# Neighbourhood attention and HGRN2 in one trunk: full-row queries for the low part of odd score tiles, and a last pair of loads in another ring

## The chip, the cores and the metric

The kernel runs on one core of a Trainium2 chip. Time is device microseconds (us) of one execution; the median of three runs before is 2596.82 us (2594.27 to 2599.92).

## What is computed

One layer of an encoder trunk over 2048 tokens of width 1024 (a grid of 32 rows by 64 columns). A modulated layer norm gives `h`; one projection gives the inputs of two branches; their outputs pass one output projection, a residual and a final layer norm. The branch that the change touches most is the neighbourhood attention of 16 heads of 64 channels:

```python
proj = h @ w_in[l]
...
q_row = lax.dynamic_index_in_dim(q, r, axis=2, keepdims=False).reshape(B, H, nqb, NA_KC, dh)
s = jnp.einsum('bhjqd,bhrjcd->bhjqrc', q_row, k_blk).astype(jnp.float32) * scale
...
s = jnp.where(col_mask[:, :, None, :], s + bias[None], -jnp.inf)
p = jax.nn.softmax(s.reshape(B, H, nqb, NA_KC, KR * NA_SPAN), axis=-1)
o = jnp.einsum('bhjqrc,bhrjcd->bhjqd', p, v_blk)
```

The other branch is a bidirectional gated recurrence (HGRN2) of 8 heads of 128 channels, computed in chunks, with an RMS norm and a gate on each head's output.

## The kernel before

**Precision.** An fp32 factor is split into a high part, rounded to fp32r, and the low rest, so that a product takes three matmuls: high by high, high by low, low by high.

**Phases.** The tokens are worked on in two halves of 1024. First the attention of the first half runs, woven with its projections (phase `n0`). Then come the 8 heads of HGRN2, twice (phase `h`): `hgrn` is the work of a head, `hgrn_tail` its rest, which is done one head later. The tail of the last head, with `u == 7` in the second half, runs beside `border_dense`: the projections of head pair 0 of the attention's second half, and before and after them a value projection `vproj` (L291, evacuated by ScalarE at L299). Then comes the attention of the second half (phase `n1`), 8 pairs of heads, `p` = 0 to 7, and at last the output projection (phase `wo`).

**The tail of a head.** In the second half the last state `R` is split into `Rh` and `Rl`, and for each group `g` of 512 tokens of the first half four tiles are loaded: `qh`, `ql`, `o1` and `sg`, all from the ring `cl`, which has four buffers. Three matmuls (L690) give what is added to `o1` (L691, VectorE). `rms_out` squares it (L345, ScalarE), splits the square (L347, L349, VectorE), sums over channels by two matmuls with ones (L354, L355), and scales (L357 to L361). The loads of `g == 1` use the buffers that `g == 0` has left: `o1` the one that L359 reads last, `sg` the one that L361 reads last.

**A score tile.** In the second half a pair has 12 tiles: row groups `R` = 1, 2, 3 (512 queries each) by column blocks `j` = 0 to 3. A tile has two heads (`hh`). A head's 64 channels fill half of the partitions; `KA`, `KB` and `Q` hold the high parts in one half and copies or low parts in the other, so that one matmul over all 128 rows (L1055) gives high by high and low by high. What is missing is the low part of the keys, `KL`. In tiles with even `j` the query operand is `Z`, which holds one head's high queries in 64 rows and zeros in the other 64, so that a matmul over all 128 rows (L1060) gives that head's term alone. In tiles with odd `j` the two heads use 64 rows each (L1062): 64 rows of `Q` and of `KL`, one head in the upper rows and one in the lower. `Z` exists once. `alone` (L780, two copies by ScalarE) refills it for the next row group right after the scores of `j == 2`.

**What follows a tile.** VectorE adds the bias and finds the extreme (L1071), ScalarE takes the exponential (L1076), VectorE divides (L1080, L1081). TensorE transposes the result (L1104), VectorE and ScalarE copy that to SBUF (L1108, L1110), and after each odd tile TensorE forms the weighted sums for two earlier tiles (L1126): pairs of matmuls, each with 64 columns of the array for one head. The gated result goes to `yv` (L1136) and to DRAM (L1137).

**Order of the work.** `weave` steps two generators: `natten_woven` (scores, transposes, sums) and a stream of dense projections (L278 with 512 columns, weights split at L814 and L815). For pair 7 the dense stream is the beginning of the output projection (L1547 to L1549); its weights are loaded at L1502 in pair 6 and in pair 7, and split by ScalarE and VectorE (L1507, L1508); the values of `y` are loaded at L1513 and split at L1539, L1540. `prep_now` and `prep_next` say after which of the 12 tiles a preparation is issued: key pieces (L992 to L994), queries (L976 to L979), values (L1003), gates (L1010, L340, L341, L1012), bias tables. TensorE's order is to be that of the code; ScalarE, VectorE and the DMA queue on SyncE (SP) are put in order by a scheduler, from priorities and its own estimate of when things are ready, except for rows pinned by hand.

Of the kernel before, what the change touches and what calls it, by code (L numbers as in the profile page):

```python
# [11 lines left out]
F32R = mybir.dt.float32r  # L12
# [26 lines left out]
def body(ctx: ExitStack, tc: tile.TileContext, t):  # L39
# [48 lines left out]
    def nm(s):  # L88
        cnt[0] += 1
        return f"{s}_{cnt[0]}"  # L90

    def tl(tag, dt=F32, shape=None):
        if tag in cur["smap"]:
            tag = cur["smap"][tag]
            return sh.tile([P, 512], dt, tag=tag, name=nm(tag), bufs=SH[tag])
        return cur["pool"].tile([P, 512] if shape is None else shape, dt, tag=tag, name=nm(tag), bufs=cur["bufs"].get(tag, 1))
# [4 lines left out]
    def ps(tag="mx"):  # L101
        if tag == "pj":
            return pp.tile([P, 512], F32, tag=tag, name=nm("pj"))
        tag = cur["map"].get(tag, tag)
        return cur["psum"].tile([P, 512], F32, tag=tag, name=nm("ps"), bufs=cur["ps"][tag])
# [237 lines left out]
    def rms_out(u, g, o_sb, sg, tok, rest=False):  # L343
        sq = tl("t")
        act.activation(sq, o_sb, AF.Square)  # L345
        sh_ = tl("rh", F32R)
        dve.tensor_copy(sh_, sq)  # L347
        sl_ = tl("rl", F32R)
        dve.tensor_tensor(sl_, sq, sh_, op=ALU.subtract)  # L349
        yield  # L350
        if rest:
            yield
        pss = ps("ss")
        pe.matmul(pss, ones, sh_, start=True, stop=False)  # L354
        pe.matmul(pss, ones, sl_, start=False, stop=True)  # L355
        r = tl("t")
        act.activation(r, pss, AF.Ln, scale=1.0 / 128.0, bias=eps_rms)  # L357
        act.activation(r, r, AF.Exp, scale=-0.5)
        dve.tensor_mul(r, r, o_sb)  # L359
        yv = tl("t")  # L360
        dve.tensor_tensor(yv, r, sg, op=ALU.mult)  # L361
        dma(yT[u][:, tok:tok + 512], yv)
# [60 lines left out]
    def hgrn(u, half, st, tail):  # L423
# [203 lines left out]
        for _ in tail:  # L627
            pass
        return hgrn_tail(u, half, sgs, ubs, decs, qibs, os_, decb_all)

    HSUM = 54

    def hgrn_tail(u, half, sgs, ubs, decs, qibs, os_, decb_all):

        R = None
        if half == 0:
            ds_ = tl("dsuf", shape=[P, 8])
            pool.memset(ds_[:, 7:8], 1.0)
            for b in range(6, -1, -1):
                dve.tensor_mul(ds_[:, b:b + 1], ds_[:, b + 1:b + 2], decb_all[:, b + 1:b + 2])  # L640
        obs = {}
        for g in (1, 0):
            po = os_[g]
            pend = []
            for b in range(3, -1, -1):
                sl = slice(b * P, (b + 1) * P)
                if R is not None:
                    pend.append((sl, R))
                if half == 0 and g == 0 and b == 0:
                    break  # L650
                rn = tl("Sb", shape=[P, P])
                if R is None:
                    dve.tensor_copy(rn, ubs[g][:, sl])
                else:
                    dve.scalar_tensor_tensor(rn, R, decs[1, g][:, b:b + 1], ubs[g][:, sl], op0=ALU.mult, op1=ALU.add)
                R = rn
            yield
            for sl, r in pend:
                pe.matmul(po[:, sl], r, qibs[1, g][:, sl], start=False, stop=True, skip_group_check=True)
            ob = tl("t")  # L660
            act.activation(ob, po, AF.Copy)
            tk = slice(g * 512, (g + 1) * 512)
            if half == 0:
                dma(op_d[u][:, tk], ob)
                dma(sg_d[u][:, tk], sgs[g])
                qb, qh, ql = tl("t"), tl("cl", F32R), tl("cl", F32R)
                for b in range(4):
                    sl = slice(b * P, (b + 1) * P)
                    dve.tensor_scalar(qb[:, sl], qibs[1, g][:, sl], ds_[:, g * 4 + b:g * 4 + b + 1], 1.0, op0=ALU.mult, op1=ALU.mult)
                act.activation(qh, qb, AF.Copy)  # L670
                dve.tensor_tensor(ql, qb, qh, op=ALU.subtract)
                dma(qb_d[u][:, 0, tk], qh.bitcast(F32))
                dma(qb_d[u][:, 1, tk], ql.bitcast(F32))
            else:
                yield from rms_out(u, g, ob, sgs[g], HALF + g * 512, g == 0)
        if half == 1:
            Rh, Rl = tl("Sb", F32R, [P, P]), tl("Sb", F32R, [P, P])
            dve.tensor_copy(Rh, R)
            dve.tensor_tensor(Rl, R, Rh, op=ALU.subtract)
            for g in range(2):  # L680
                tk = slice(g * 512, (g + 1) * 512)
                qh, ql, o1, sg = tl("cl", F32R), tl("cl", F32R), tl("cl"), tl("cl")
                dma(qh.bitcast(F32), qb_d[u][:, 0, tk])
                dma(ql.bitcast(F32), qb_d[u][:, 1, tk])
                dma(o1, op_d[u][:, tk])
                dma(sg, sg_d[u][:, tk])
                yield
                po = ps("pc")
                for i, (a, b) in enumerate(((Rh, qh), (Rh, ql), (Rl, qh))):
                    pe.matmul(po, a, b, start=i == 0, stop=i == 2)  # L690
                dve.tensor_tensor(o1, po, o1, op=ALU.add)  # L691
                yield from rms_out(u, g, o1, sg, g * 512)
# [340 lines left out]
    class Natten:  # L1033
# [8 lines left out]
        def scores(self, R, j):  # L1042
# [8 lines left out]
            def kv(z):  # L1051
                return keys[z].rearrange("p (r c) -> p r c", c=GW)[:, k0 - self.r_base:k0 - self.r_base + nr, KC[j]:KC[j] + kw]
# [2 lines left out]
                pe.matmul(scs[hh][:, 0:nk], qs[hh], kv(("KA", "KB")[hh]), start=True, stop=False, skip_group_check=True)  # L1055
            for hh in range(2):
                hs_ = slice(hh * 64, hh * 64 + 64)
                if self.half and j % 2 == 0:
                    o = hh * 512 + j * P
                    pe.matmul(scs[hh][:, 0:nk], keys["Z"][:, o:o + P], kv("KL"), start=False, stop=True, skip_group_check=True)  # L1060
                else:
                    pe.matmul(scs[hh][:, 0:nk], qs[hh][hs_], kv("KL")[hs_], start=False, stop=True, skip_group_check=True)  # L1062
# [75 lines left out]


    def prep_now(st):  # L1140
        return {0: [(st.k, 3), (st.k, 4)], 1: [(st.q, 3), (st.gate, 2)], 2: [(st.v, 7), (st.v, 5), (st.v, 6)], 4: [(st.gate, 3), (st.table, "bot", 0)],
                6: [(st.table, "bot", 1)], 7: [(st.table, "bot", 3)]}

# [314 lines left out]
    with psum_phase("n0", NPS), tc.manual_schedule(engines={mybir.EngineType.PE}):  # L1458
        with phase("st", SB_, SMS), tc.manual_schedule(engines={getattr(mybir.EngineType, e) for e in ("PE", "SP", "Activation", "DVE")}):
            raws, feed, first = startup()  # L1460
        with phase("n0", NB0, SM0):
            natten_init(4, 0)
            st = first_half(raws, feed, first)
# [7 lines left out]
    with psum_phase("h", *HPS), phase("h", HB, SMH), tc.manual_schedule(engines={mybir.EngineType.PE}):  # L1471
        hgrn_init()
        tail = iter(())
        for i in range(16):
            half, u = divmod(i, 8)
            if i < 15:
                nxt = hgrn_dense((i + 1) % 8, (i + 1) // 8, i in (6, 7), reload if i == 6 else None)
                tail, st = weave(hgrn(u, half, st, tail), nxt, HTOT, HSUM)
# [133 lines left out]
    with psum_phase("n1", NPS), phase("n1", NB1, SM1), tc.manual_schedule(engines={mybir.EngineType.PE}):  # L1612
        natten_init(4, 1)
        st = st0
# [13 lines left out]
        for u in range(8):  # L1628
# [15 lines left out]
            st = nxt  # L1644
# [77 lines left out]
```

## Time and profile before

| what | value |
|---|---|
| median of three runs | 2596.82 us |
| the profiled execution, its own time | 2596.31 us |
| its span, from the first to the last instruction | 2594.5 us |
| mean granted TensorE clock | 0.995 of full speed |
| attention of the second half with its dense stream (`n1`), by the lines' first and last starts | about 1735 to 2280 us |
| TensorE busy in 1740 to 2270 us | 522.92 of 530 us |

Engines are PE (TensorE), PEld (its weight loads), DVE (VectorE), ACT (ScalarE), POOL (GpSimd) and SP (SyncE, which issues the DMAs). A row of the timeline has the start in us from the span's start, the duration, the engine, the line, the operation and the tiles as out<-in; `x2` means that two equal instructions in a row were merged, and brackets hold the idle time before the row and what ended it. Matmuls are pipelined: one starts while the one before it still drains, so what a matmul costs is read from start to start.

### The profile page before, as it was taken

The numbers are of one execution on the slowest core, as the hardware profiler recorded it, in microseconds if no ns is written. First come the engines' busy times: TensorE is split into PE (matmuls) and PEld (weight loads), VectorE is DVE, ScalarE is ACT, GpSimd is POOL, SyncE is SP. The second block draws the span as 40 slices with busy tenths as digits, with TensorE's granted clock in tenths as the row PEclk, the third lists the DMA queues.
The fourth block names the chain that finished last, engine by engine and source line by source line (L and its number), as shares of the span: only waits on it lengthen the run. The fifth ranks groups of instructions, "written<-read, shape, count | busy, mean of one in ns | idle before, by whom it ended". The sixth has DMA issues, their size and how long they took to land.

```text
span 2594.5 us, 46029 instructions
## 1 busy us (share of the span) xinstructions
PE 2557.3 (99%) x17196; PEld 2154.2 (83%) x17196; DVE 1752.1 (68%) x4394; ACT 1438.9 (55%) x2869; POOL 108.5 (4%) x143
## 2 busy tenths in 40 slices
PE   8999999999999999999999999999999999999998
PEld 6888888878888888888888888898888887788887
DVE  7445545387877778877888787555777778648443
ACT  5533444376666666666766666455777777531110
POOL 0000000000000000000000000000000000032221
PEclk9999999999999999999999999999999999999999
DMA  7566454212122226222222222345455556443331
GB/s 293 143 206 154 143 178 140 90 51 70 66 73 74 66 85 228 83 73 86 80 65 69 82 86 83 120 128 155 123 145 136 147 139 173 132 155 130 96 95 57
DMA packets 230527, 304.79 MB, mean 117 GB/s; under 512 B 29351, under 2 KB 118055, under 8 KB 229159
## 3 DMA queue, kind: packets, MB, share of 16 engines
q1 hardware_dynamic: 230303, 301.85, 37.9%
q8 instruction: 135, 2.21, 0.4%
q14 instruction: 89, 0.73, 0.1%
HBM read 222.37 MB, written 71.18 MB: 113 GB/s over the span
## 4 chain that ended last, share of the span: by engine, by line
PE 94%; DVE 3%; ACT 1%; DMA 1%; issue 0%; SPq 0%; DVEq 0%; ACTq 0%
PE pj L278 51%; PE pj L291 7%; PE ps L1549 4%; PE ps L1547 4%; PE ps L1548 4%; PE ps L1126 3%; PE ps L1104 3%; PE ps L482 2%; PE ps L474 2%; PE ps L1055 2%; PE ps L549 1%; PE ps L278 1%; PE ps L578 1%; PE ps L1062 1%; PE ps L580 1%; PE ps L521 1%
## 5 line engine op out<-in xcount | busy, mean ns | idle before, releaser
L278 PE MATMUL pj<-h,wh 128*128 128x512 f32 x3984 | 1264.7, 398 | 1.5 <-ACT wh L814 1.1
L278 PEld LDWEIGHTS pj<-h,wh 128*128 128x128 f32 x3984 | 721.8, 188 | 149.8 <-issue 10.5
L278 PE MATMUL pj<-h,wl 128*128 128x512 f32 x1992 | 780.3, 392 | 0.0
L278 PEld LDWEIGHTS pj<-h,wl 128*128 128x128 f32 x1992 | 373.8, 188 | 82.4 <-DVE wl L815 0.4
L1076 ACT ACTIVATE pbuf<-pbuf,mx 128x480 f32<-128x480 f32 (+5 forms) x256 | 152.5, 597 | 107.5 <-DVE mx L1071 106.4
L291 PE MATMUL pj<-wh,h 128*128 128x256 f32 x1024 | 197.1, 287 | 2.2 <-ACT vt L299 2.0
L1071 DVE CUSTOM_DVE_ANT_1 pbuf<-ps,bias 128x480 f32<-128x480 f32 (+5 forms) x256 | 129.1, 540 | 98.8 <-PE ps L1062 42.1
L291 PEld LDWEIGHTS pj<-wh,h 128*128 128x128 f32 x1024 | 164.6, 193 | 6.0 <-ACT vt L299 3.3
L269 DVE TENSOR_TENSOR wl<-wr,wh 128x512 fp32r<-128x512 f32 x192 | 131.4, 685 | 46.2 <-ACT wh L268 45.9
L268 ACT ACTIVATE wh<-wr 128x512 fp32r<-128x512 f32 x192 | 120.3, 626 | 73.1 <-PE pj L278 66.7
L291 PE MATMUL pj<-wl,h 128*128 128x256 f32 x512 | 145.6, 284 | 0.0
L1110 ACT ACTIVATE pt<-ps 120x384 f32<-120x384 f32 (+3 forms) x128 | 65.2, 510 | 120.1 <-PE ps L1104 119.9
L1104 PE MATMUL ps<-ident,pbuf 128*128 128x128 f32 (+2 forms) x832 | 112.9, 273 | 4.7 <-DVE pbuf L1081 3.9
L1108 DVE COPY pt<-ps 120x384 f32<-120x384 f32 (+3 forms) x128 | 74.9, 585 | 62.5 <-PE ps L1104 61.6
L1104 PEld LDWEIGHTS ps<-ident,pbuf 128*128 128x128 f32 (+2 forms) x832 | 96.6, 136 | 22.7 <-ACT pbuf L1076 2.5
L468 DVE TENSOR_TENSOR de<-e,de 128x512 f32<-128x512 f32 x64 | 44.2, 691 | 92.9 <-ACT de L467 92.9
L1523 ACT ACTIVATE yh<-yr 128x512 fp32r<-128x512 f32 x52 | 32.7, 628 | 132.4 <-PE ps L1548 115.2
L1596 DVE TENSOR_TENSOR vt<-ps,gt 128x512 f32<-128x512 f32 x24 | 16.5, 692 | 129.9 <-PE ps L1549 129.9
L1081 DVE TENSOR_SCALAR pbuf<-pbuf,mx 128x480 f32<-128x480 f32 (+5 forms) x256 | 101.0, 412 | 3.7
L788 ACT ACTIVATE e<-pj 128x512 f32<-128x512 f32 x97 | 57.8, 596 | 78.9 <-PE pj L278 72.0
L291 PEld LDWEIGHTS pj<-wl,h 128*128 128x128 f32 x512 | 98.8, 193 | 1.0
L840 DVE TENSOR_TENSOR wl<-wr,wh 128x512 fp32r<-128x512 f32 x68 | 46.9, 691 | 69.4 <-ACT wh L839 64.3
(289 smaller groups left out, 4771.2 us busy)
## 6 DMA issues: line engine op xcount, KB each, us to landing
wr<-in_w_in SPq DMA_DIRECT2D x276, 256.0 KB
yr<-yq SPq DMA_DIRECT2D x64, 256.0 KB
bias<-tint SPq DMA_DIRECT2D x24, 480.0 KB
x<-in_x SPq DMA_DIRECT2D x32, 256.0 KB
ada<-in_ada_m SPq DMA_DIRECT2D x8, 1024.0 KB
wr<-in_w_v SPq DMA_DIRECT2D x32, 256.0 KB
nv<-vt SPq DMA_DIRECT2D x32, 256.0 KB
hs<-s SPq DMA_DIRECT2D x32, 256.0 KB
```

Source lines behind the costliest of these rows:

```text
L268: act.activation(hi, raw, AF.Copy)
L269: dve.tensor_tensor(lo, raw, hi, op=ALU.subtract)
L278: pe.matmul(pz, a, b, start=(k == 0 and n == 0), stop=(k == KT - 1 and n == 2))
L291: pe.matmul(pzs[tp][:, i * 256:(i + 1) * 256], a, b, start=(k == 0 and n == 0 and i == 0), stop=(k == KT - 1 and n == 2), skip_group_check ...
L1071: return dve.tensor_tensor_reduce(s[:, 0:nk].rearrange("p (r c) -> p r c", c=kw), sc[:, 0:nk].rearrange("p (r c) -> p r c", c=kw), bt[:, 0 ...
L1076: act.activation(s[:, 0:nk], s[:, 0:nk], AF.Exp, scale=-1.0, bias=mx[:, 0:1], accum_out=mx[:, 1:2])
L1081: dve.tensor_scalar(s[:, 0:nk], s[:, 0:nk], mx[:, 2:3], 1.0, op0=ALU.mult, op1=ALU.mult)
L1104: pe.transpose(ptp[0:cw, c * P:(c + 1) * P], s[:, c * cw:(c + 1) * cw], ident)
L1126: pe.matmul(self.po[R][hs_, j * P:(j + 1) * P], v[:, hh * 64:hh * 64 + 64], pts[hh][0:n * KW[j], c * P:(c + 1) * P], start=(c == 0), stop= ...
L1547: pe.matmul(pz, yh[:, kk], wh, start=first, stop=False)
L1548: pe.matmul(pz, yh[:, kk], wl, start=False, stop=False)
L1549: pe.matmul(pz, yl[:, kk], wh, start=False, stop=last)
```

## The change

There are three edits. In the tail of the last head (`u == 7`, `g == 1`) `o1` and `sg` come from the ring `de`, which has two buffers, instead of `cl`. In the second half the odd tiles take the low part with `Z` over all 128 rows, as the even tiles do. For pair 7 `prep_now` issues the gate of row group 2 after tile 3 instead of 1, the queries of row group 3 after tile 5 instead of 1, and the gate of row group 3 after tile 6 instead of 4.

```diff
-                qh, ql, o1, sg = tl("cl", F32R), tl("cl", F32R), tl("cl"), tl("cl")
+                qh, ql = tl("cl", F32R), tl("cl", F32R)
+                o1, sg = (tl("de" if u == 7 and g else "cl") for _ in range(2))
...
-                if self.half and j % 2 == 0:
+                if self.half:
                     o = hh * 512 + j * P
                     pe.matmul(scs[hh][:, 0:nk], keys["Z"][:, o:o + P], kv("KL"), start=False, stop=True, skip_group_check=True)
...
     def prep_now(st):
+        if st.p == 7:
+            return {0: [(st.k, 3), (st.k, 4)], 2: [(st.v, 7), (st.v, 5), (st.v, 6)], 3: [(st.gate, 2)], 4: [(st.table, "bot", 0)], 5: [(st.q, 3)],
+                    6: [(st.gate, 3), (st.table, "bot", 1)], 7: [(st.table, "bot", 3)]}
```

`alone` is left where it was, after the scores of `j == 2`. So in the changed kernel the tile `j == 3` reads a `Z` that already holds the queries of the next row group (except in the very last row group): its product of queries and the keys' low part is taken with other queries than the reference's.

In the changed kernel the lines behind the first edit are numbered one higher (L1060 becomes L1061), and those behind the last edit four higher (L1507 becomes L1511).

The first place is the DMA queue (SP) in the tail of the last head; `cl_18684` to `cl_18687` are the loads for `g == 0`, `cl_18763` on those for `g == 1`, and `wr` are weights of the value projection. Before:

```order
L683 DMA cl_18684<-qb 128x512
L684 DMA cl_18685<-qb 128x512
L685 DMA cl_18686<-op 128x512
L362 DMA yq<-t_18289 128x512
L686 DMA cl_18687<-sgd 128x512
...
L683 DMA cl_18763<-qb 128x512
L684 DMA cl_18764<-qb 128x512
L262 DMA wr_19208<-in_w_v 128x512
L262 DMA wr_19214<-in_w_v 128x512
L685 DMA cl_18765<-op 128x512
L362 DMA yq<-t_18760 128x512
L686 DMA cl_18766<-sgd 128x512
```

And in the changed kernel:

```order
L684 DMA cl_18684<-qb 128x512
L685 DMA cl_18685<-qb 128x512
L686 DMA de_18765<-op 128x512
L687 DMA de_18766<-sgd 128x512
L686 DMA cl_18686<-op 128x512
L362 DMA yq<-t_18289 128x512
L687 DMA cl_18687<-sgd 128x512
...
L684 DMA cl_18763<-qb 128x512
L685 DMA cl_18764<-qb 128x512
L262 DMA wr_19208<-in_w_v 128x512
L262 DMA wr_19214<-in_w_v 128x512
L362 DMA yq<-t_18760 128x512
```

The two loads for `g == 1` have moved from behind two weight loads to a place ahead of the `o1` of `g == 0`. On TensorE the two matmuls with ones that belong to them move too: L354 stands three rows earlier, and L355 17 rows earlier.

The second place is ScalarE in pair 6, where the queries of pair 7 (`Q_24634`, `Q_24635`), a key piece (`e_24334`) and the first weights of the output projection (`vt_24410`, `vt_24412`, `vt_24487`, `vt_24489`) are split between a copy of a transposed tile (L1110) and the exponential of a score tile (L1076). Before:

```order
L1110 ACTIVATE pt_24539<-ps_24534 128x512
L992 ACTIVATE KA_3615_18865<-e_24334 64x256
L992 ACTIVATE KB_3616_18866<-e_24334 64x256
L1507 ACTIVATE wo_24710<-vt_24487 128x512
L1507 ACTIVATE wo_24714<-vt_24489 128x512
L976 ACTIVATE Q_24634<-e_24187 64x512
L977 ACTIVATE Q_24635<-e_24187 64x512
L1507 ACTIVATE wo_24640<-vt_24410 128x512
L1507 ACTIVATE wo_24644<-vt_24412 128x512
L1076 ACTIVATE pbuf_18861,mx_24572<-pbuf_18861,mx_24572 128x360
```

And in the changed kernel:

```order
L1111 ACTIVATE pt_24539<-ps_24534 128x512
L977 ACTIVATE Q_24634<-e_24187 64x512
L993 ACTIVATE KA_3615_18865<-e_24334 64x256
L978 ACTIVATE Q_24635<-e_24187 64x512
L1511 ACTIVATE wo_24640<-vt_24410 128x512
L1511 ACTIVATE wo_24644<-vt_24412 128x512
L993 ACTIVATE KB_3616_18866<-e_24334 64x256
L1511 ACTIVATE wo_24710<-vt_24487 128x512
L1511 ACTIVATE wo_24714<-vt_24489 128x512
L1077 ACTIVATE pbuf_18861,mx_24572<-pbuf_18861,mx_24572 128x360
```

The same eight rows stand between the two; the queries and the older weights (`vt_24410`, `vt_24412`) now come before the younger ones (`vt_24487`, `vt_24489`). VectorE's rows for the same tiles move alike.

The third place is ScalarE at the start of pair 7, where `prep_now` has its new table; `Q_25074` and `Q_25075` are the queries of row group 3, and the three `sg` are the gates of row groups 1, 2 and 3. Before:

```order
L992 ACTIVATE KA_3615_18865<-e_24334 64x256
L992 ACTIVATE KA_3615_18865<-e_24779 64x512
L992 ACTIVATE KB_3616_18866<-e_24334 64x256
L992 ACTIVATE KB_3616_18866<-e_24779 64x512
L976 ACTIVATE Q_25074<-e_24620 64x512
L977 ACTIVATE Q_25075<-e_24620 64x512
L1076 ACTIVATE pbuf_18861,mx_24885<-pbuf_18861,mx_24885 128x288
...
L1010 ACTIVATE sg_24933<-bk_24344 128x512
L1010 ACTIVATE sg_25080<-e_24471 128x512
L1010 ACTIVATE sg_25312<-e_24929 128x512
```

And in the changed kernel:

```order
L993 ACTIVATE KA_3615_18865<-e_24334 64x256
L993 ACTIVATE KA_3615_18865<-e_24779 64x512
L977 ACTIVATE Q_25379<-e_24620 64x512
L993 ACTIVATE KB_3616_18866<-e_24334 64x256
L993 ACTIVATE KB_3616_18866<-e_24779 64x512
L978 ACTIVATE Q_25380<-e_24620 64x512
L1077 ACTIVATE pbuf_18861,mx_24885<-pbuf_18861,mx_24885 128x288
...
L1011 ACTIVATE sg_24933<-bk_24344 128x512
L1011 ACTIVATE sg_25238<-e_24471 128x512
L1011 ACTIVATE sg_25432<-e_24929 128x512
```

The buffers have later numbers, since the code issues them later, but in ScalarE's queue the same rows stand between the same neighbours: only one `Q` row has passed two key rows.

## The prediction

> **What bounds the kernel now.** I read the page first: the span, the busy shares of the engines and the chain of work that ended last. Then I asked who waits on TensorE.
>
> ```profile
> span 2594.5 us, 46029 instructions
> PE 2557.3 (99%) x17196; PEld 2154.2 (83%) x17196; DVE 1752.1 (68%) x4394; ACT 1438.9 (55%) x2869; POOL 108.5 (4%) x143
> ...
> PE 94%; DVE 3%; ACT 1%; DMA 1%; issue 0%; SPq 0%; DVEq 0%; ACTq 0%
> ```
>
> TensorE is busy for 99% of the span and makes up 94% of the chain. So an edit can change the time in two ways only: by what TensorE itself takes from start to start, and by the few places where it stands still. The four largest entries in the list of TensorE's waits between 1700 and 2400 us are these:
>
> ```profile
> PE ps L1104 <- DVE pbuf L1081: 3.9, 2, 2.1
> PE pj L291 <- ACT vt L299: 2.0, 2, 1.8
> PE pj L1547 <- ACT yh L1539: 1.2, 1, 1.2
> PE pj L278 <- ACT wh L814: 1.1, 1, 1.1
> ```
>
> The columns are the sum in us, the number of waits and the longest. Together they make 8.2 us, so what the two edits that move work can gain in this stretch lies within that; the edit to the scores is a matter of TensorE's own rows.
>
> **The scores of the odd tiles.** The forms and counts of L1062 are those of the second half alone, and four rows of the timeline show how a tile with even `j` and one with odd `j` run at 480 columns, four more at 288:
>
> ```profile
> L1062 PE MATMUL ps<-KL,Q x96: 393/437/488, 1742.1 to 2271.0; 64*128 64x480 f32 x32, 64*128 64x360 f32 x32, 64*128 64x384 f32 x16, 64*128 64x288 f32 x16
> ...
> 1980.26 0.38 PE L1055 MATMUL ps<-KA,Q 128*128 128x480 f32 x1
> 1980.48 0.38 PE L1055 MATMUL ps<-KB,Q 128*128 128x480 f32 x1
> 1980.70 0.61 PE L1060 MATMUL ps<-KL,Z 128*128 128x480 f32 x2
> 1981.14 0.63 PE L278 MATMUL pj<-h,wh 128*128 128x512 f32 x2
> ...
> 1974.08 0.38 PE L1055 MATMUL ps<-KA,Q 128*128 128x480 f32 x1
> 1974.30 0.38 PE L1055 MATMUL ps<-KB,Q 128*128 128x480 f32 x1
> 1974.61 0.49 PE L1062 MATMUL ps<-KL,Q 64*128 64x480 f32 x2
> 1975.03 0.44 PE L1126 MATMUL ps<-pt,V 128*64 128x128 f32 x4
> ...
> 1991.00 0.29 PE L1055 MATMUL ps<-KA,Q 128*128 128x288 f32 x1
> 1991.53 0.63 PE L278 MATMUL pj<-h,wh 128*128 128x512 f32 x2
> ...
> 2005.16 0.30 PE L1055 MATMUL ps<-KA,Q 128*128 128x288 f32 x1
> 2005.84 0.44 PE L1126 MATMUL ps<-pt,V 96*64 96x128 f32 x4
> ```
>
> The even tile of 480 columns takes 1981.14 - 1980.26 = 0.88 us, four streams of 0.22. The odd one takes 1975.03 - 1974.08 = 0.95 us. Its two matmuls over 64 rows run side by side: both are over 0.49 us after the first began, and the next row starts 0.42 us after them. That saves a stream of 0.22 us, but it is paid for twice: the step from L1055 into the 64-row form is 1974.61 - 1974.30 = 0.31 instead of 0.22, and the step out of it 0.42 instead of 0.22. So the full-row form looks 0.07 us cheaper at 480 columns, and at 288 it is 0.53 against 0.68, which is 0.15 cheaper.
>
> That comparison is not fair yet. An odd tile is followed by the weighted sums (L1126), whose matmuls use 64 columns of the array, an even one by dense work. What a full-array matmul pays before L1126 is shown at the end of the stage:
>
> ```profile
> 2276.54 0.39 PE L1548 MATMUL pj<-wo,yh 128*128 128x512 f32 x1
> 2276.77 0.40 PE L1549 MATMUL pj<-wo,yl 128*128 128x512 f32 x1
> 2277.10 0.44 PE L1126 MATMUL ps<-pt,V 128*64 128x128 f32 x4
> ```
>
> From L1548 to L1549 it is 0.23 us, from L1549 to L1126 0.33: the step into the sums costs 0.10 us more. An odd tile in the new form would thus take 0.88 + 0.10 = 0.98 at 480 columns, 0.03 more than now, and 0.53 + 0.10 = 0.63 at 288, 0.05 less. On a straight line between these, 384 columns give 0.01 less and 360 give 0.02 less. With two matmuls to a tile the counts are 16, 16, 8 and 8 tiles at 480, 360, 384 and 288 columns: 16 x 0.03 - 16 x 0.02 - 8 x 0.01 - 8 x 0.05 = -0.32 us. Starts are printed to a hundredth, so 48 tiles leave about 0.5 us on either side. **This edit is worth about -0.3 us (-0.8 to +0.2).** The Trainium skill, "TensorEngine Tiling (Array Packing)", Key Properties, says that a change of tiling mode drains TensorE; this trace agrees, with 0.09 to 0.20 us a change. By that rule alone the edit, which takes one of three changes from each of 48 tiles, would gain 5 to 10 us; the same page's Theoretical Speedup allows up to twice the speed where the contraction is 64 long or less, and by that alone the edit would lose the 8.6 us of the first rival below.
>
> **The wait that it adds.** The odd tiles now read `Z`, and for `j == 3` that is the `Z` that ScalarE refills after `j == 2`. So 46 of these matmuls get a wait on ScalarE (23 refills, two heads), and behind it in TensorE's queue stand the sums and the dense stream. The tightest of the 23 refills is in pair 6:
>
> ```profile
> 2189.98 1.27 ACT L780 ACTIVATE Z<-Q 64x512 fp32r<-64x512 f32 x2
> ...
> 2193.42 0.40 PE L1062 MATMUL ps<-KL,Q 64*128 64x288 f32 x2
> ```
>
> The refill ends at 2191.25, and the matmul that will need it starts at 2193.42: 2.2 us of room. In pair 7 the queries that the refill copies are issued later by the code, but the scheduler leaves their rows between the same neighbours. I cost the wait at nothing; what hides it is the dense work between tiles 2 and 3.
>
> **The loads for the last head.** The wait on L299 is this one; the rows are TensorE, then SyncE, VectorE and ScalarE:
>
> ```profile
> 1709.69 0.86 PE L690 MATMUL ps<-cl,Sb 128*128 128x512 f32 x3
> 1713.14 0.28 PE L291 MATMUL pj<-wh,h 128*128 128x256 f32 x1
> 1715.23 0.38 PE L291 MATMUL pj<-wh,h 128*128 128x256 f32 x1 [1.81 <-ACT vt L299]
> ...
> 1709.20 0.33 SPq L685 DMA_DIRECT2D cl<-op  x1
> ...
> 1708.48 0.69 DVE L359 TENSOR_TENSOR t<-t,cl 128x512 f32<-128x512 f32 x1 [0.55 <-ACT t L358]
> 1713.34 0.69 DVE L691 TENSOR_TENSOR cl<-ps,cl 128x512 f32<-128x512 f32 x1 [2.08 <-PE pj L291]
> ...
> 1714.06 0.63 ACT L345 ACTIVATE t<-cl 128x512 f32<-128x512 f32 x1 [3.54 <-DVE cl L691]
> 1714.60 1.07 ACT L299 ACTIVATE vt<-pj 128x512 f32<-128x512 f32 x2
> ```
>
> Read backwards: TensorE has no free PSUM buffer until L299 has emptied one; L299 stands in ScalarE's queue behind L345, which waits for L691. L691 names TensorE as its releaser, but L690 was over at 1710.55; it is the load of `o1` that came late. That load was issued at 1709.20, right when L359 had finished with the buffer (1709.17). In the changed kernel it goes to a buffer of `de` and is issued ahead of the first group's `o1`, some 40 us earlier. Then L691 can start at 1710.55, when its matmuls are done, L345 ends at about 1711.9, and L347 at about 1712.5, with one weight split put behind L691 on VectorE. ScalarE is free when the value projection ends. L354, which the scheduler has moved ahead, finds its operand at 1712.5 and starts right behind the row of 1713.14, at about 1713.3; its own time was spent later before, so it adds nothing. What had started at 1715.23 starts about 1713.3: **-2.0 us**. Late next is L299 itself, whose evacuation overlaps L354. Ends: 0, if something else holds ScalarE, and -2.0.
>
> **The order in pair 6.** The two waits on L1081 are at 2180.84 and 2202.70. ScalarE and VectorE before the first:
>
> ```profile
> 2174.79 0.63 ACT L1507 ACTIVATE wo<-vt 128x512 fp32r<-128x512 f32 x1 [1.89 <-DMA vt<-in_w_out]
> 2177.68 0.58 ACT L1076 ACTIVATE pbuf<-pbuf,mx 128x360 f32<-128x360 f32 x1
> ...
> 2172.24 0.98 DVE L1081 TENSOR_SCALAR pbuf<-pbuf,mx 128x480 f32<-128x480 f32 x2
> 2175.45 0.69 DVE L1508 TENSOR_TENSOR wo<-vt,wo 128x512 fp32r<-128x512 f32 x1 [0.72 <-ACT wo L1507]
> 2179.42 0.22 DVE L1080 RECIPROCAL mx<-mx 128x1 f32<-128x1 f32 x2
> ...
> 2180.84 0.62 PE L1104 MATMUL ps<-ident,pbuf 128*120 128x128 f32 x4 [2.12 <-DVE pbuf L1081]
> ```
>
> ScalarE stood still for 1.89 us until a weight tile had landed, and VectorE for 0.72 behind it. In the new order that tile's split comes last of the eight, so other work fills the time. ScalarE gains up to 1.9 us. VectorE's nine rows between L1081 and L1080 took 2179.42 - 2173.22 = 6.2 us; without the 0.72, and without a tenth or two before it, they take about 5.3. VectorE decides, since L1080 stands behind them: **-0.9 us** (0 to -1.9). The second wait, at 2202.70, has unbroken work on both engines before it, and there the same rows stand in the same place: the new table for pair 7 moves the code's order, not the queue's. I cost that edit at nothing. What hides it is the scheduler's own hoisting; if it did act, the wait of 1.74 us there is what it could take away, or double.
>
> **The sum.** -0.3 - 2.0 - 0.9 = -3.2 us, from 2596.3 for the profiled execution to 2593.1. The median of the runs is 0.5 us above that execution, so the forecast is 2593.6.
>
> **Rivals.** *Packing pays in full.* The gaps around the 64-row pair might not go away with it: a step out of scores into sums may cost 0.20 us whatever stands before, as it does now. Then each odd tile loses a whole stream, 0.22, 0.18, 0.165 and 0.13 us at the four widths: 16 x 0.22 + 8 x 0.18 + 16 x 0.165 + 8 x 0.13 = 8.6 us, and with the other two terms 2596.8 - 2.9 + 8.6 = 2602.5, slower. It makes the kernel slower as soon as less than 5.7 of the 48 x 0.19 = 9.1 us of gaps go away. The Trainium skill, "TensorEngine Tiling (Array Packing)", Theoretical Speedup, speaks for it with its factor of two. Against it stand the even tiles, which stream without a gap, and the 0.10 us from L1549 to L1126. *Drain-free.* If the step from `Z` into the sums cost nothing, 47 x 0.10 = 4.7 us more would be gained: 2588.9. Against it: the same row at 2277.10. *Moves without effect.* The two stalls may come back elsewhere, the one at 1715 as a wait of the first score tiles for key copies, the one at 2180 as a longer one at 2202. Then only -0.3 is left: 2596.5. For it speaks that VectorE and ScalarE are full before 2202; against it that no wait of a score tile is in the list, and that these rows hang on TensorE's own progress and shift with it.
>
> **How the numbers follow.** Forecast 2593.6: 65%. Moves without effect: 17%. Drain-free: 10%. Packing pays in full: 6%. Something else: 2%. The range of 8 in 10 takes in the forecast with its bounds and the runs' own spread, the third rival, and part of the second: 2589 to 2598.5. About 0.2%, 5.2 us, is what a measurement of this kernel can tell from no change. Below 2591.6 lie most of drain-free and a fifth of the forecast: 22%. Above 2602.0 lie most of the first rival and little else: 5%. Within: 73%.
>
> **What would show it.** Right: L1061 at 288 to 480 columns with rows of `Z` for all 192 matmuls and steps of about 0.13 to 0.22 us; 0.10 us more before the sums; the loads into `de` issued near 1665 us and no wait on L299 above 0.3 us; the wait near 2180 shortened to about 1.2 us, the one near 2202 unchanged. Wrong: a wait of L1061 on ScalarE in the list; steps before the sums of 0.2 us above the stream; a new wait near 1735 us.

## The result, and the profile after

| | before | changed |
|---|---|---|
| median | 2599.13 us (6 runs, 2594.27 to 2601.97) | 2589.77 us (6 runs, 2589.64 to 2590.92) |
| the profiled execution: own time, span | 2596.31, 2594.5 us | 2589.64, 2587.8 us |
| mean granted TensorE clock of that execution | 0.995 | 0.997 |

The changed kernel takes 0.9972 of the time before (95% interval 0.9961 to 0.9983), about 7 us less; the interval reaches to a gain of less than 0.2%. The two medians lie 9.4 us apart, but the larger sets of runs of the kernel before further down, with medians of 2596.78 to 2597.59 us, speak for the 7 us. Repeated beside other kernels the ratio was 0.9973 (0.9963 to 0.9984), 2590.26 us. The forecast was 2593.6 us, in a range of 2589 to 2598.5, and a change within 0.2% had been given 73%.

I first asked again who waits on TensorE between 1700 and 2400 us. This is the list of the changed kernel, with sum, number and longest wait in us:

```profile
PE ps L1105 <- DVE pbuf L1082: 3.4, 3, 1.9
PE pj L1551 <- ACT yh L1543: 1.2, 1, 1.2
PE pj L278 <- ACT wh L815: 1.1, 1, 1.1
PE ps L1105 <- DVE mx L1081: 0.8, 2, 0.4
```

The entry for L299 is gone, and no entry of L1061 on ScalarE has come: both as forecast. The place of the old wait, in the timeline of the changed kernel (TensorE, SyncE, VectorE, ScalarE):

```profile
1706.89 0.86 PE L691 MATMUL ps<-cl,Sb 128*128 128x512 f32 x3
1710.46 0.39 PE L354 MATMUL ps<-rh,ones 128*128 128x512 f32 x1
...
1657.52 0.34 SPq L686 DMA_DIRECT2D de<-op  x1
...
1707.79 0.69 DVE L692 TENSOR_TENSOR de<-ps,de 128x512 f32<-128x512 f32 x1 [0.69 <-DMA wr<-in_w_v]
...
1708.52 0.63 ACT L345 ACTIVATE t<-de 128x512 f32<-128x512 f32 x1 [0.79 <-DVE de L692]
1709.94 1.32 ACT L299 ACTIVATE vt<-pj 128x512 f32<-128x512 f32 x2 [0.79 <-PE pj L291]
```

The load is issued some 50 us ahead of its use, L692 starts when its matmuls are done (1706.89 + 0.86 = 1707.75; its brackets name a weight tile that landed then), and L299 now waits for TensorE instead of TensorE for L299.

To see where the 6.7 us between the two spans came from, I compared the starts of the same matmul in both, one after the other. Five steps hold nearly all of it: -1.3 us between 91 and 95 us, -1.5 between 562 and 566 us, -3.95 between 1706 and 1735 us, -0.35 over the attention's pairs 0 to 5, +0.4 from there to the end. The first two lie in code that is the same in both kernels. They show in a table of stretches (length, then busy time with the number of instructions for PE, PEld, DVE, ACT and POOL, then the granted clock, the DMA share and GB/s), first of the kernel before, then of the changed one:

```profile
91.25:94.66 3.41, 3.41 (x11) 2.73 (x10) 0.56 (x1) 1.58 (x3) 0.00 (x0) 0.50 0.43 153
558.88:562.29 3.41, 0.61 (x4) 0.21 (x2) 3.34 (x10) 2.79 (x6) 0.00 (x0) 1.00 0.02 8
562.30:565.70 3.40, 3.40 (x16) 3.40 (x17) 3.40 (x8) 0.00 (x0) 0.00 (x0) 0.50 0.03 5
```

```profile
91.25:94.66 3.41, 3.25 (x20) 2.71 (x19) 1.28 (x3) 2.70 (x6) 0.00 (x0) 1.00 0.41 152
555.88:559.29 3.41, 2.39 (x11) 1.66 (x9) 3.41 (x9) 2.63 (x5) 0.00 (x0) 1.00 0.30 88
559.29:562.70 3.41, 1.60 (x14) 1.63 (x15) 3.34 (x10) 1.70 (x3) 0.00 (x0) 1.00 0.00 0
562.30:565.70 3.40, 3.40 (x21) 2.95 (x20) 3.40 (x10) 1.55 (x3) 0.00 (x0) 1.00 0.00 0
```

Both kernels let TensorE stand still for most of 558 to 562 us, and for 1.5 us just before 91 us. In the execution of before the clock granted afterwards is 0.50 for 3.4 us, in the other one it is 1.00. Such a stretch costs about half its length, 1.7 us. Neither of these two comes from the edits: the changed kernel's other profile has the one at 562 us, and of all 14 profiles only those of `before` and `e7` have the one at 91 us. The last section shows how far it can be told whether a stretch follows. At 1716 us it was the edit that took it away. The kernel before, ahead of, in and behind its stall there:

```profile
1713.00:1715.20 2.20, 0.42 (x4) 0.22 (x2) 1.14 (x3) 1.14 (x3) 0.00 (x0) 1.00 0.66 213
1715.90:1719.40 3.50, 3.50 (x18) 3.48 (x17) 0.69 (x1) 0.28 (x1) 0.00 (x0) 0.51 0.71 206
1719.40:1723.00 3.60, 3.60 (x31) 3.56 (x30) 1.34 (x3) 2.68 (x5) 0.00 (x0) 1.00 0.05 18
```

The busy share reads full in both of the last two rows, but 18 matmuls pass in one and 31 in the other. The 3.95 us are thus the stall, about 2 us, and the half clock behind it, 1.6 to 1.9 us. All five kernels whose waits on L299 at this place sum to 2.0 us or more show the stretch behind them; the nine without that stall do not. The granted clock of every run agrees: its mean is 0.9962 over the 94 runs of the kernel before further down and 0.9975 over 13 of the changed kernel. Times 2595 us that is an estimated 3.4 us less lost to the clock, of 7.1 us between the mean times.

### The profile page after: what moved, and what is told of

Its sections match the earlier page's. It is cut to its first block, busy times and chain, and to the rows that moved or that the text cites. A ratio compares the mean times of both kernels' runs of the same rounds, so it can differ in the third digit from the quotient of the medians.

```text
span 2587.8 us, 46020 instructions
## 1 busy us (share of the span) xinstructions
PE 2552.1 (99%) x17196; PEld 2157.0 (83%) x17196; DVE 1751.9 (68%) x4394; ACT 1435.8 (55%) x2869; POOL 107.6 (4%) x143
## 4 chain that ended last, share of the span: by engine, by line
PE 91%; DMA 3%; DVE 3%; ACT 1%; issue 0%; SPq 0%; DVEq 0%
PE pj L278 50%; PE pj L291 7%; PE ps L1551 4%; PE ps L1552 4%; PE ps L1553 4%; PE ps L1127 3%; PE ps L1105 3%; PE ps L482 2%; DMA bias<-tint 2%; PE ps L474 2%; PE ps L1056 1%; PE ps L549 1%; PE ps L278 1%; PE ps L578 1%; PE ps L580 1%; PE ps L521 1%
## 5 line engine op out<-in xcount | busy, mean ns | idle before, releaser
L1072 DVE CUSTOM_DVE_ANT_1 pbuf<-ps,bias 128x480 f32<-128x480 f32 (+5 forms) x256 | 128.9, 539 | 98.3 <-PE ps L1061 60.6
L1111 ACT ACTIVATE pt<-ps 120x384 f32<-120x384 f32 (+3 forms) x128 | 65.0, 508 | 121.1 <-PE ps L1105 121.0
```

The lines of the kernel that those rows point to most:

```text
L1072: return dve.tensor_tensor_reduce(s[:, 0:nk].rearrange("p (r c) -> p r c", c=kw), sc[:, 0:nk].rearrange("p (r c) -> p r c", c=kw), bt[:, 0 ...
```

## The experiments

The experiments came in three groups, each with runs of the kernel before on its own chip; their medians of before are 2597.59, 2597.29 and 2596.78 us. All ratios are against these. `e2`, `e4` and `e7` carry over the displaced queries of the tile `j == 3`.

### The three edits one by one

The ring alone (`e1_de_only`):

```diff
+                o1, sg = (tl("de" if u == 7 and g else "cl") for _ in range(2))
```

> Only the ring of the last head's two loads is changed. Theory 1 (the gain is the wait at the end of the recurrence, 2.0 us, and the stretch of half clock that followed it in the profiled execution before, 3.4 us at half speed, about 1.6 us): 3 to 4 us faster than before, no wait on L299 over 0.3 us, granted clock 1.00 around 1710 to 1720 us. Theory 2 (the full-row tiles bring the gain): within 2 us of before. Theory 3 (the difference is the spread of the runs of before): no difference of the medians beyond that spread.

It took 2594.39 us, ratio 0.9989 (0.998 to 0.9997). No wait on L299 is left. But TensorE has a stall that neither theory had, at 2207 us; timeline, ScalarE and TensorE:

```profile
2206.13 0.63 ACT L1508 ACTIVATE wo<-vt 128x512 fp32r<-128x512 f32 x1 [2.08 <-DMA vt<-in_w_out]
2206.66 0.47 ACT L1111 ACTIVATE pt<-ps 96x384 f32<-96x384 f32 x1
...
2207.18 0.32 PE L1127 MATMUL ps<-pt,V 96*64 96x128 f32 x1 [1.55 <-ACT pt L1111]
```

ScalarE waits for a weight tile; the copy that the sums need stands behind that split. Half clock follows:

```profile
2207.50:2210.90 3.40, 3.40 (x16) 2.59 (x11) 2.71 (x10) 2.03 (x6) 0.00 (x0) 0.50 0.92 193
```

The full rows alone (`e2_fullrow_only`):

```diff
-                if self.half and j % 2 == 0:
+                if self.half:
```

> Only the odd tiles are changed; as in the changed kernel, the tile j = 3 reads queries of the next row group in its low part. Theory 1: the rows themselves -1 us, the order in pair 6 -0.8 us, some of it given back at transposes: 0 to 2 us faster than before, and the wait on L299 of 1.8 us still there. Theory 2: 5 us faster or more. The packing rival: 5 us slower or more.

It took 2598.41 us, ratio 1.0006 (0.9998 to 1.0015): not faster. Its profile is of the slowest of its 11 executions, 2602.69 us. There the same blocked copy is the largest entry of the list of TensorE's waits, as the weight tile came later still (ScalarE waited 7.23 us for it):

```profile
PE ps L1126 <- ACT pt L1110: 5.0, 1, 5.0
```

The table for pair 7 alone (`e3_prep_only`):

```diff
     def prep_now(st):
+        if st.p == 7:
+            return {0: [(st.k, 3), (st.k, 4)], 2: [(st.v, 7), (st.v, 5), (st.v, 6)], 3: [(st.gate, 2)], 4: [(st.table, "bot", 0)], 5: [(st.q, 3)],
+                    6: [(st.gate, 3), (st.table, "bot", 1)], 7: [(st.table, "bot", 3)]}
```

> Only the table of pair 7 is changed. The scheduler leaves the same rows between the same neighbours, so theory 1 expects the waits near 2180, 2202 and 2250 us unchanged and the time within 1 us of before. A theory that the late preparation relieves ScalarE expects the wait near 2202 us (1.7 us) to go and 2 to 4 us.

It took 2595.24 us, ratio 0.9989 (0.9981 to 0.9997), and its profile, of the fastest of its 12 executions, has no stall near 2207 us, though those near 1712 and 2176 us are both there. So the edit that I had cost at nothing is worth about as much as the ring.

Full rows and table without the ring (`e4_no_de`): both edits above.

> The changed kernel without the ring edit, with the same displaced queries in j = 3. Theory 1: 3 to 4 us slower than the changed kernel, 0 to 2 us faster than before. Theory 2: as fast as the changed kernel, 7 us faster than before.

It took 2594.38 us, ratio 0.999 (0.9981 to 0.9999). Its wait near 2178 us is 1.3 us long where the table alone has 2.6; the time is the same as the table's alone. The ring is what separates this kernel from the changed one.

### The changed kernel again, and without the full rows

The changed kernel once more (`e5_changed_again`):

> The changed kernel itself, beside the three others of this set. With the ring edit worth about 3 us, and the other two together about 3 us in the first set: 6 to 7 us faster than before (ratio near 0.9975).

Ring and table, odd tiles as before (`e6_even_tiles_only`):

```diff
-                if self.half:
+                if self.half and j % 2 == 0:
```

> The changed kernel with the old odd tiles (64 rows each), so ring and table alone. New theory: ring and table bring the time, by waits, and the rows of the odd tiles are worth 1 us, so within 1.5 us of the changed kernel, with the wait near 2178 us back at 2.5 to 3 us. Rival: the full-row tiles are needed for the gain, 3 us or more slower than the changed kernel.

2590.26 us for the changed kernel, and 2590.81 us, ratio 0.9972 (0.9963 to 0.9982), for ring and table alone. The edit to the scores is worth nothing that can be measured; the other two together are the whole gain. The wait near 2174 us, which I had expected back at 2.5 to 3 us, was 1.3 us here too, so it does not hang on the full rows. The same kernel was run once more as the base of the last group (`e9_even_tiles_again`):

> Ring and table alone, with the odd tiles as before, once more, as the base for the two runs behind it. Every theory: the same as the first time, a ratio of 0.997 to the kernel before, 2589 to 2592 us.

2590.29 us, ratio 0.9975 (0.9966 to 0.9985).

### All tiles with 64 rows

Here even and odd tiles take the low part over 64 rows each, otherwise as in the changed kernel (`e8_all_tiles_64_rows`):

```diff
-                if self.half:
+                if False:
```

> The changed kernel with the 64-row pairs in all tiles of the second half, even ones too. By steps (a pair saves a stream but pays 0.09 us going in and 0.2 us before dense work, and the next matmul 0.1 us): 0.17 us more at 480 columns to 0.27 at 288 for each of the 48 even tiles, about 10 us, so 9 to 12 us slower than the changed kernel. By packing alone (a stream saved in each of 96 tiles): 8 to 17 us faster.

It took 2596.34 us, ratio 1.0 (0.9991 to 1.0009), 6.1 us more than the changed kernel beside it. Timeline of an even tile of 480 columns, followed by dense work:

```profile
1977.91 0.38 PE L1056 MATMUL ps<-KA,Q 128*128 128x480 f32 x1
...
1978.44 0.49 PE L1063 MATMUL ps<-KL,Q 64*128 64x480 f32 x2
1978.87 0.73 PE L278 MATMUL pj<-h,wh 128*128 128x512 f32 x2
```

The tile takes 1978.87 - 1977.91 = 0.96 us, the full-row form 0.88. That packing gains is excluded by its sign. The loss is below the 9 to 12 us that I had expected, but not because a tile was priced wrongly. Over pairs 0 to 5, with 36 even tiles, this kernel takes 2136.48 - 1735.58 = 400.90 us and the changed one 394.00: 0.19 us a tile, within the 0.17 to 0.27 expected. Pairs 6 and 7 give some of it back, with 141.7 us to the last sums against 144.4 and 143.5 in the two profiles of the changed kernel: the waits near 2180 and 2202 us are only 0.75 and 1.0 us long.

### Pair 7's gates and queries, late on ScalarE

If the table helped by taking preparations out of ScalarE's way, holding them back should help more (`e7_pinned_late`, on the changed kernel):

```diff
-            keep = pinned if raw is self.bk.get("q") or self.first else lambda x: x
+            keep = pinned if raw is self.bk.get("q") or self.first or (self.half and self.p == 7 and R == 3) else lambda x: x
...
-            keep = pinned if raw is self.bk.get("g") or self.first else lambda x: x
+            keep = pinned if raw is self.bk.get("g") or self.first or (self.half and self.p == 7) else lambda x: x
```

> The changed kernel with the late preparations of pair 7 (gates of row groups 2 and 3, queries of row group 3) pinned on ScalarE to the place where the code issues them. If these rows are what is in the way before the wait on L1082 near 2195 us (1.9 and 0.4 us): that wait goes or falls under 0.7 us, and the time falls by 2 to 4 us against the changed kernel. If the wait only moves to a later tile: within 1 us of the changed kernel.

It took 2592.08 us, ratio 0.9985 (0.9976 to 0.9993), 1.8 us more than the changed kernel beside it, which is within the two intervals. The wait that I aimed at, near 2199 us, fell to 0.4 us; these stand in its place in the list of waits:

```profile
PE ps L1105 <- DVE mx L1081: 1.9, 1, 1.9
...
PE pj L1551 <- ACT wo L1511: 1.5, 1, 1.5
```

These waits end near 2144 and 2225 us, and half clock follows each. The first is not the work of the pinning: the second profile of ring and table alone (`e9` above), in which nothing is pinned, has it too, with 1.9 us and half clock behind it, and in both profiles VectorE has just waited over 4.5 us for a bias tile (L1072). The second is a weight split that now comes too late, behind the pinned rows. Holding the preparations back brought no gain, and the place of the splits matters.

### The order of the weight splits alone

So the last test of the table leaves it out. On the ring alone, the split of two weight tiles that landed long ago (6 and 7) is called ahead of that of two late ones (0 and 1), as the scheduler puts them with the new table (`e11_split_order`):

```diff
-                extra = {0: [(wo_load, 1, 2, 3)], 1: [(wo_split, 1, 0, 1), (wo_load, 1, 6, 7)], 2: [(wo_split, 1, 2, 3, 4, 5)], 3: [(wo_split, 1, 6, 7)]}
+                extra = {0: [(wo_load, 1, 2, 3)], 1: [(wo_load, 1, 6, 7), (wo_split, 1, 6, 7), (wo_split, 1, 0, 1)], 2: [(wo_split, 1, 2, 3, 4, 5)]}
```

> The ring alone, with the old table for pair 7, but the output projection's weight tiles 6 and 7 of the second column half are split ahead of tiles 0 and 1, in tile 1 of pair 7. So ScalarE has the tiles that landed long ago ahead of the copy of the transposed tile (L1111), and those that land late behind it, as with the new table; no preparation is moved. If the table works through this order of the splits alone (my theory): no wait of L1127 near 2207 us, where the ring alone has 1.8 us; the late tiles now hold up two rows of ScalarE behind that copy instead, which have about 1.5 us to spare, so the time is 1.8 to 3.5 us below the ring alone, a ratio of 0.997 to 0.998. If the table gains by taking the preparations out of the way: no change against the ring alone, 0.9985 to 0.999.

It took 2590.7 us, ratio 0.9976 (0.9967 to 0.9985), where the ring alone had 0.9989 (0.998 to 0.9997) and ring with table 0.9975 beside it. ScalarE in its timeline:

```profile
2202.94 0.62 ACT L1508 ACTIVATE wo<-bk 128x512 fp32r<-128x512 f32 x1
2203.46 0.47 ACT L1111 ACTIVATE pt<-ps 96x384 f32<-96x384 f32 x1
2203.83 0.62 ACT L1508 ACTIVATE wo<-bk 128x512 fp32r<-128x512 f32 x1
2204.35 1.19 ACT L1508 ACTIVATE wo<-vt 128x512 fp32r<-128x512 f32 x2
```

The copy L1111 has a tile that is there (`bk`) ahead of it and the late ones (`vt`) behind it; no row waits, and TensorE has no stall near 2207 us. The profiled execution even has a stall of 2.7 us near 2175 us, against 1.3 with the table. The intervals of this kernel and of the ring alone just touch (0.9985 and 0.998) and come from two groups, so the times alone would be thin evidence. The queues add to it: behind 1655 us, ScalarE's rows of ring and table (`e9`) stand, by the names of their tiles, in the order of the ring alone, but for the splits of four weight tiles near 2204 to 2226 us, where two that are there (`bk`) have changed places with two late ones (`vt`); SyncE's order does not differ at all. The same holds for the table alone against the kernel before. The table moves no preparation in ScalarE's queue, so its gain cannot come from that.

### A stall put back

To price a stall with what follows it, ring and table alone get six more squares by ScalarE, into the same tile, ahead of L299 (`e10_stall_back`):

```diff
-        act.activation(sq, o_sb, AF.Square)
+        for _ in range(7 if late else 1):
+            act.activation(sq, o_sb, AF.Square)
```

> Ring and table alone, and ScalarE squares o1 of the last group seven times instead of once (the six more cost it about 3.1 us ahead of L299 and of the operand of the sums with ones). It puts back, by another cause, a stall of TensorE near 1712 us of 2.3 to 2.8 us, and changes nothing else. If a stall costs its own length alone: 2.3 to 2.8 us more than ring and table alone in the same call, and full clock behind it. If a stall of that length is followed by a stretch at half clock (my theory): a window of 3.4 us with a granted clock of 0.5 behind it in the profile, which costs up to 1.7 us more, so 3 to 4.5 us more in all, and the gain of the ring is gone. If TensorE's end does not hang on this place at all: 0.

It took 2598.87 us, ratio 1.0005 (0.9997 to 1.0014), against 2590.29 us and 0.9975 for its base: 8.6 us more. The entry of L299 in the list of its waits, then two stretches of its profile, then the same two of the base's:

```profile
PE pj L291 <- ACT vt L299: 4.0, 2, 3.7
```

```profile
1711.00:1715.00 4.00, 0.61 (x6) 0.41 (x4) 0.88 (x2) 3.72 (x7) 0.00 (x0) 1.00 0.46 103
1715.00:1718.50 3.50, 3.18 (x14) 3.09 (x15) 0.93 (x2) 0.75 (x2) 0.00 (x0) 0.51 0.52 181
```

```profile
1711.00:1715.00 4.00, 4.00 (x34) 3.90 (x33) 1.76 (x4) 3.76 (x7) 0.00 (x0) 1.00 0.71 214
1715.00:1718.50 3.50, 3.50 (x31) 3.50 (x31) 3.27 (x6) 3.33 (x8) 1.04 (x2) 1.00 0.51 146
```

The stall is longer than I had expected, 3.85 us from start to start, since L299 stands behind all seven squares. Behind it the same matmuls fall back by another 1.9 us, in the half-clock stretch. That is 5.8 us; the two profiled executions differ by 6.1. The medians differ by 2.5 us more, about the width of one interval (0.0009 of the time is 2.3 us). The clocks of all runs point the same way: the mean is 0.9961 here and 0.9977 for the base, an estimated 4 us more lost to the clock (0.0016 x 2595), where the profiled execution lost 1.9 us behind the stall. Where these other stretches lie is not shown. That a stall costs its own length alone is ruled out by the profile.

### The odd tile's own queries

The refill of `Z` is put after the scores of `j == 3`, so that every odd tile takes its own queries (`e12_queries_right`):

```diff
-            if st.half and j == 2 and (R < 3 or nxt):
+            if st.half and j == 3 and (R < 3 or nxt):
```

> The changed kernel with the refill of Z put after the scores of the odd tile j == 3 instead of after j == 2, so that the odd tiles' low part is taken with their own queries. ScalarE's two copies now stand between the tiles j == 3 and j == 0 of the next row group, and the matmul that needs the new Z comes one tile later than the refill, as before. If which queries Z holds has no part in the time: that of the changed kernel, 2589 to 2592.5 us, a ratio of 0.9972 +- 0.001. If the tighter place of the refill makes TensorE wait: a wait of L1061 on ScalarE in the list of waits, up to 0.3 us for each of 23 refills, 3 to 7 us more.

It took 2592.36 us, ratio 0.9983 (0.9974 to 0.9992), inside the band of the first reading, but the profile shows something that neither had: no wait of L1061 on ScalarE, two on loads near 2190 us (1.2 and 0.6 us), and one of 5.1 us near 2205 us. Its entry in the list of waits:

```profile
PE pj L1553 <- DVE yl L1544: 5.1, 1, 5.1
```

The wait near 2199 us is gone in exchange. VectorE's split of `y` stands behind a row of L1072 that waits 7.9 us for a bias tile, up to 2205.5 us; what made that load late is open. Over pairs 0 to 5 this kernel takes 392.68 us, 1.3 us less than the changed one, so the place of the refill is not quite without effect. As the full rows bring nothing, the kernel to keep is ring and table alone: every tile has its own queries, and its time is that of the changed kernel.

## Why the prediction was right in sign and too small

**The scores of the odd tiles: right, and gone on the way.** An odd tile of 480 columns and one of 288 in the changed kernel:

```profile
1967.06 0.38 PE L1056 MATMUL ps<-KA,Q 128*128 128x480 f32 x1
...
1967.50 0.61 PE L1061 MATMUL ps<-KL,Z 128*128 128x480 f32 x2
1968.04 1.64 PE L1127 MATMUL ps<-pt,V 128*64 128x128 f32 x26
...
1998.12 0.30 PE L1056 MATMUL ps<-KA,Q 128*128 128x288 f32 x1
1998.38 0.42 PE L1061 MATMUL ps<-KL,Z 128*128 128x288 f32 x2
1998.73 0.44 PE L1127 MATMUL ps<-pt,V 96*64 96x128 f32 x4
```

0.98 and 0.61 us, where 0.98 and 0.63 were forecast. Over all tiles the medians went from 0.956 to 0.980 us at 480 columns, 0.782 to 0.743 at 360, 0.823 to 0.803 at 384 and 0.683 to 0.617 at 288: with the counts 0.38 - 0.62 - 0.16 - 0.53 = -0.93 us. Two matmuls at the ends of pairs 0 to 5 show what was left of it, first in the kernel before, then in the changed one:

```profile
1741.59 0.39 PE L1055 MATMUL ps<-KA,Q 128*128 128x480 f32 x1
...
2135.94 1.11 PE L1104 MATMUL ps<-ident,pbuf 128*96 128x128 f32 x6
```

```profile
1734.84 0.39 PE L1056 MATMUL ps<-KA,Q 128*128 128x480 f32 x1
...
2128.84 1.18 PE L1105 MATMUL ps<-ident,pbuf 128*96 128x128 f32 x6
```

394.35 us between them before, 394.00 after: -0.35 us. That this equals the forecast's -0.3 is luck in part, since the forecast was of the tiles themselves, which gained -0.93; the rest was given back in small steps at the transposes. The difference returns in other profiles: between the two matmuls it is 394.0 us in four profiles of kernels with full rows and table, 394.4 to 394.6 in the seven with the old tiles, but also 394.4 with the full rows alone. The runs without this edit are as fast. "Packing pays in full" and "Drain-free" both fell.

**The ring: right, but only half of its price.** The stall of 2 us went as forecast. I read the stall off the list of waits and did not ask what TensorE's clock does behind it. The half-clock stretch at 1716 us stood in the profile of before; with it the term is -3.6 to -3.9 us in the profiled execution, where I had -2.0. Alone, the ring measured 0.9989, some -3 us with an interval from -0.8 to -5, the new stall at 2207 us included.

**The table: the step that failed.** It reads: "the new table for pair 7 moves the code's order, not the queue's. I cost that edit at nothing." The rows that I had compared were those near the wait at 2202 us, and those do stay. Some rows further on the queue does change. Before, in the profile of before, and in the changed kernel (ScalarE):

```profile
2208.72 0.63 ACT L1507 ACTIVATE wo<-vt 128x512 fp32r<-128x512 f32 x1 [2.20 <-DMA vt<-in_w_out]
2209.26 0.47 ACT L1110 ACTIVATE pt<-ps 96x384 f32<-96x384 f32 x1
```

```profile
2199.22 0.61 ACT L1511 ACTIVATE wo<-bk 128x512 fp32r<-128x512 f32 x1
2199.74 0.47 ACT L1111 ACTIVATE pt<-ps 96x384 f32<-96x384 f32 x1
...
2208.71 1.14 ACT L1511 ACTIVATE wo<-vt 128x512 fp32r<-128x512 f32 x2
```

ScalarE's wait of 2.2 us for the weights stood in the trace, ahead of a copy that TensorE needs, and I passed it over because TensorE did not wait there. In that execution TensorE was itself late, since a half-clock stretch begins at 2204 us; in the ring alone it was not, and waited 1.5 us. The full rows alone has such a stretch too, at 2202.7 us, but there the weight tile came so late that TensorE waited 5.0 us all the same. That cover is my reading of the traces; that other executions of the kernel before have the wait in its place is not shown, and between the two profiles the table alone gains only the 1.7 us of that stretch here. That the order of the splits is what counts, the run with that order alone and the queues show. Alone the table gives 0.9989 (0.9981 to 0.9997); beside the ring it takes away the new stall that the ring uncovers.

**The order in pair 6: right in size, and without weight.** The first wait there, in the changed kernel, with VectorE's rows that decide it:

```profile
2173.68 0.84 PE L1105 MATMUL ps<-ident,pbuf 128*120 128x128 f32 x6 [1.32 <-DVE pbuf L1082]
...
2165.76 0.98 DVE L1082 TENSOR_SCALAR pbuf<-pbuf,mx 128x480 f32<-128x480 f32 x2
2172.26 0.22 DVE L1081 RECIPROCAL mx<-mx 128x1 f32<-128x1 f32 x2
```

1.32 us instead of 2.12, -0.8 where -0.9 was forecast; VectorE's rows in between take 2172.26 - 2166.74 = 5.5 us instead of 6.2. The wait near 2202 us stayed, as forecast, and two steps of about 0.5 us came, near 2141 and 2217 us, so that pairs 6 and 7 together are 0.4 us longer. A kernel with a wait of 2.7 us at this place (the split order alone) is as fast as those with 1.3. Nor does it take the new order to shorten this wait: ring and table alone has the old order and 1.3 us, since ScalarE waits only 0.35 us for the weight tile; in the ring alone and the split order alone ScalarE waits 2.4 and 2.5 us, and TensorE 2.6 and 2.7.

**The added wait on Z: right.** Nothing waits for it, with own queries or with displaced ones.

**The sum.** Forecast -3.2 us, measured about -7. What was missing is the half clock behind the stall, some 1.7 us, and the table, some 2.4 us alone. The rest is within the intervals. The stated range of 2589 to 2598.5 us holds the measured 2589.77, but by luck: its lower end was drawn for part of "Drain-free" (2588.9 us), which the steps of the tiles exclude. "Moves without effect" fell for the ring, and held for the order in pair 6.

## What to carry to other kernels

Price a stall of the bounding engine with the clock that it is granted afterwards, not by its length alone, and read the count of matmuls in the stretch behind it, since busy time does not show it. Where an edit feeds a scheduler, follow the whole queue to the end of the phase and look for rows that move past one that waits for a DMA: such a wait cost nothing here while TensorE was late, and 1.5 us and a stretch of half clock once an earlier stall was mended.

## What the runs showed of the hardware

A stretch at a granted clock of 0.5 lasts 3.41 us here, or twice that (the one at the very end of an execution aside), and it begins on a grid: within one execution the beginnings lie whole multiples of 3.413 us apart. In the profile of before they are at 91.25, 562.29, 1715.99 and 2204.10 us, 138, 338 and 143 such steps; in other executions the grid lies elsewhere. I divided all 14 profiles into the pieces of their grids, from 20 to 2560 us, and took for each piece that ran at full clock the idle time of TensorE in it (its length less the busy time that the profile gives). No piece with less than 0.9 us was followed by half clock; the others:

| idle time of TensorE in a piece | pieces | followed by half clock |
|---|---|---|
| 0.9 to 1.4 us | 58 | 0 |
| 1.4 to 1.8 us | 18 | 3 |
| 1.8 to 2.1 us | 13 | 10 |
| 2.1 us and more | 17 | 17 |

So it is not the length of a stall alone that counts, but how much of it falls into one piece. The 2.8 us of idle time near 559 us, which every kernel has, are followed by half clock in 10 of 14 profiles: in these ten 2.2 us or more lie in one piece, in the other four at most 1.94. In the first tables of stretches above it is 2.80 us in the kernel before (3.41 - 0.61), against 1.02 and 1.81 us in two pieces in the changed one. The least idle time that half clock followed is 1.46 us, near 89 us, in two of seven profiles; what decides between 1.4 and 2.1 us stays open. The Trainium skill, "TensorE: Matmul & The Clock Gate", HAM oscillation — how this bites in real kernels, gives the rule that no idle gap should be over about 3.4 us; here about half that length was at times enough, and the measurement decides. Its Part 1 states a window of 3413 ns that runs freely and does not start again with the kernel; the trace agrees, with its steps of 3.413 us and with a grid that lies elsewhere in each execution. Part of the spread between executions of one kernel goes with the clock: the 35, 28 and 31 runs of the kernel before spread over 7 to 11 us, and a mean clock lower by 0.001 goes with 1.0 to 1.2 us more time, which accounts for a third to under a half of the variance.
